# A two-layer hybrid block on one core: the first modulation in quarters and column groups, raw weights issued on ScalarE's queue, and a last tile whose second half comes in two parts

## The chip, the core and the metric

The kernel runs as one program on one core of a Trainium2 chip. Five engines work there from queues of their own, each in the order in which its instructions stand: TensorE (PE, with its weight loads as PEld), VectorE (DVE), ScalarE (ACT), GpSimd (POOL) and SyncE (SP). They wait for one another by semaphores. An instruction that waits holds everything behind it on its engine, and that goes for an instruction that issues a DMA too. The metric is the device time of one execution in microseconds (us). Before the change it is 3673.63 us, the median of three runs (3672.63 to 3673.88).

## The reference

Two layers (`DEPTH` 2) over 2048 latent and 256 context tokens of 1024 values each. Cut to what matters here:

```python
silu_c, silu_cc = jax.nn.silu(c), jax.nn.silu(c_ctx)
for l in range(DEPTH):
    mod_lat = silu_c @ w_ada[l] + b_ada[l]        # (1, 3*1024): shift, scale, gate
    mod_ctx = silu_cc @ w_ada[l] + b_ada[l]
    x, ctx = _layer(x, ctx, mod_lat, mod_ctx, ...)
return _rms_norm(x, g_final)

# _layer:
sh, sc, gt = jnp.split(mod_lat, 3, axis=-1)
xn = _rms_norm(x, g_norm) * (1 + sc[:, None]) + sh[:, None]
(au, av, az, bq, bk, bv, bz, cq, ck, cv, co, cz, cg) = _split_proj(xn @ w_in)
# gated MLP on (au, av, az), attention on (bq, bk, bv, bz), mLSTM on (cq, ck, cv, co, cz, cg)
x = x + gt[:, None] * (jnp.concatenate([y_a, y_b, y_c], axis=-1) @ w_out)
```

Nothing can be projected before the shift and the scale of layer 0 are known: they are two products of a vector of 1024 with 2048 columns of `w_ada[0]`, 8 MB in all.

## The kernel before, in words

The tokens are 18 tiles of 128 (2 of context, 16 latent). Per layer there are three phases: the projection (`proj_phase`, about 0 to 890 us and 1912 to 2680 us), the attention (`attn_phase`), and the output projection (`out_phase`, 1695 to 1912 us and from 3457 us). The instructions are written as Python generators; a scheduler that works with a timeline of its own then sets the order on each engine, so an edit moves instructions that it doesn't name.

**Projection.** Three macros of six tiles each; in each macro seven groups of columns of `w_in` (c1, c3, c2, a1, a2, b1, b2), 8 chunks of 128 rows per group (k = 0 to 7). A chunk is loaded as `raw` (three buffers, `wload`), and split into a rounded part and a rest (`split_w`, L197 to L204: CAST on ACT and subtraction on DVE, for a quarter of the chunks both on POOL) into one of 11 `w` buffers. A tile takes 24 matmuls of 512 columns per group (`gemm`, L209). Four of a group's eight `w` buffers come free halfway through the group's last tile. After its matmuls a tile is evacuated by ACT and DVE, and the results go to DRAM with `ld` on SP's queue; `put_blocks` writes a transposed block as four small DMAs (to `sct`, `sy`, `sk`, `sq`). Late in each projection phase the mLSTM (`ml_state`, `ml_out`) runs between the matmuls.

**All loads on one queue.** `ld` (L51 to L58) issues on SP: weights, tokens, `w_ada`, rope tables (`tab`), and nearly all stores.

**The first modulation.** `mod_load(0, h)` loads `w_ada[0]` in two halves h of 4 MB, eight DMAs of 512 KB each, into the later `xn` buffers. `mod_first(0, h)` multiplies: `silT` holds the two silu vectors, two columns per k. In half 0 the shift's columns are summed on DVE (`mod_sum`, L401 and L403) and the scale's on PE; in half 1 both are on PE (L384: 24 matmuls of 512 columns with a stationary operand of two columns, two profile records each). The rows are then copied, transposed back (L395) and finished by `mod_fin`. The first three tiles are normalised ahead (`make_xn`): per half, four transposes, then scale and shift of four blocks of 128 columns, CAST and subtraction.

**Other modulations.** `mod_job` sums `w_ada` of layer 1 and the gates on DVE, from 64 loads of 256 KB (`mst`, three buffers). These loads and the `tab` loads are written inside `tc.issue_after(lastw[0])`: they may not be put ahead of the last weight load that has been written, as far as both are on one engine.

**Output.** `out_phase` gives two matmul groups of 512 columns per tile; in the last layer then the gate, the residual, a Square with a sum, the inverse root on POOL (three instructions) and two multiplications on DVE, each followed by a store.

Of the kernel before, what the change touches and what calls it, by code (L numbers as in the profile page):

```python
# [12 lines left out]
ALU = mybir.AluOpType  # L13
# [22 lines left out]
def hybrid_kernel(ctx: ExitStack, tc: tile.TileContext, x, c, ctxt, c_ctx, w_ada, b_ada, g_norm, w_in, w_s, b_s,  # L36
# [135 lines left out]
    silT = const([P, KC, 2], "silT")  # L172
# [39 lines left out]
    def out_phase(l):  # L212
        last = l == DEPTH - 1

        with ExitStack() as st:
# [61 lines left out]
            for ti, i in enumerate(tiles):  # L277
# [7 lines left out]
                ss = pt([P, 2], "ss", 3) if last else None  # L285
                for g in range(2):
                    cs = slice(g * 512, (g + 1) * 512)
                    acc = pacc()
                    gemm(acc, xs, ws[g], 0, 512)
                    V.tensor_tensor(xnew[:, cs], acc, gt[s][:, cs], op=ALU.mult)  # L290
                    (V if last else G).tensor_tensor(xnew[:, cs], xnew[:, cs], xo[:, cs], op=ALU.add)
                    if last:
                        A.activation(xo[:, cs], xnew[:, cs], AF.Square, accum_out=ss[:, g:g + 1])
                if not last:
                    nc.gpsimd.dma_start(xres[i], xnew)
                else:
                    rs = pt([P, 1], "rs", 3)
                    G.tensor_tensor(rs, ss[:, 0:1], ss[:, 1:2], op=ALU.add)
                    rsqrt(rs, rs, 1.0 / D, EPS, 1)
                    for g in range(2):  # L300
                        cs = slice(g * 512, (g + 1) * 512)
                        V.scalar_tensor_tensor(xnew[:, cs], xnew[:, cs], rs, gfin[:, cs], op0=ALU.mult, op1=ALU.mult)
                        ld(out[0, (i - NCT) * P:(i - NCT + 1) * P, cs], xnew[:, cs])

    def proj_phase(l):
        with ExitStack() as st:
# [29 lines left out]
            def silu_prep():  # L336
# [9 lines left out]
                V.tensor_copy(silT, tr[:, 0:16].rearrange("p (s k) -> p k s", s=2))  # L346
# [19 lines left out]
            def mod_load(l, h):  # L366

                src = w_ada[l, :, 0:2 * D].rearrange("(k p) (g h c) -> k p g h c", p=P, g=2, h=2)
                for k in range(KC):
                    if k % 2 == 0:  # L370
                        t = xns[AHEAD + k // 2 % (half + 1 - AHEAD)]().bitcast(F32)
                        mraw.append(t.rearrange("p a k t -> p (a k t)").rearrange("p (q g c) -> p q g c", q=2, g=2))
                    raw = mraw[-1][:, k % 2]
                    gate[0] = ld(raw, src[k, :, :, h, :]).ins

            def mod_first(l, h, rT):

                tr = pm()
                accs = [pacc() for _ in range(1 + h)]
                vacc = [] if h else [pt([P, 520], "mkv", 3) for _ in range(2)]  # L380
                for k in range(KC):
                    raw = mraw[(h * KC + k) // 2][:, k % 2]
                    for j, acc in enumerate(accs):
                        T.matmul(acc[0:2], silT[:, k, :], raw[:, 1 - j], start=(k == 0), stop=(k == KC - 1))  # L384
# [905 lines left out]
```

## Time and profile before

| what | us |
|---|---|
| median of three runs | 3673.63 |
| the profiled execution | 3684.58 |
| its span, first to last instruction | 3682.9 |
| PE busy in the span | 3582.6 |
| DVE, ACT, POOL busy | 2556.9, 1942.0, 1892.3 |

The profiled execution is 10.95 us longer than the median of the runs, and 1.7 us of it lie outside the span. A line of the profile names the line of the code, the engine, the operation, and what it writes and reads (`out<-in`); an idle time is put down to what ended it. PE's busy time is modelled from the starts of pipelined matmuls, so that how far two matmuls start apart says more than how long one lasts. A matmul of full-precision operands (L384, L777, L830) leaves two records.

### The profile page before, as it was taken

How to read it: one execution, taken by the hardware profiler on the slowest of the kernel's cores; microseconds unless marked ns; L12 is line 12 of the kernel's file. 1: busy time of each engine (PE TensorE's matmuls, PEld its weight loads, DVE VectorE, ACT ScalarE, POOL GpSimd, SP SyncE). 2: the span in 40 equal slices, each digit the busy share in tenths (PEclk: the TensorE clock that was granted, in tenths of full speed). 3: DMA queues.
4: the chain of work that ended last, by engine and by line, in shares of the span. 5: the costliest groups of instructions: out<-in, count | busy, mean ns of one | idle time of the engine just before them, and what ended most of it. 6: DMA issues, size and time to landing. Idle time of an engine off the chain costs nothing.

```text
span 3682.9 us, 58371 instructions
## 1 busy us (share of the span) xinstructions
PE 3582.6 (97%) x19405; PEld 2937.3 (80%) x19405; DVE 2556.9 (69%) x6341; ACT 1942.0 (53%) x3409; POOL 1892.3 (51%) x2448
## 2 busy tenths in 40 slices
PE   8999999998999999999999999999999999999999
PEld 4877778776888888887788788877778888888787
DVE  4676664778888888887324636466888888888754
ACT  4223243334878788786114432432377877777621
POOL 2241342454777777776322524244557777777610
PEclk9999999999999999999999999999999999999999
DMA  7456455576001011002545553557720101100143
GB/s 216 137 138 175 138 129 136 159 194 156 25 28 37 17 35 43 24 12 95 175 121 151 132 148 83 141 145 180 174 57 18 31 27 35 35 24 10 58 148 113
DMA packets 531690, 359.21 MB, mean 98 GB/s; under 512 B 297274, under 2 KB 432178, under 8 KB 531388
## 3 DMA queue, kind: packets, MB, share of 16 engines
q1 hardware_dynamic: 518172, 336.05, 33.8%
q10 hardware_dynamic: 10368, 9.52, 0.8%
q0 software_dynamic: 2848, 9.91, 0.7%
q8 instruction: 154, 2.52, 0.3%
q14 instruction: 148, 1.21, 0.1%
HBM read 269.56 MB, written 85.76 MB: 96 GB/s over the span
## 4 chain that ended last, share of the span: by engine, by line
PE 69%; DMA 6%; DVE 4%; POOL 3%; issue 2%; SPq 2%; ACT 2%; DVEq 0%; POOLq 0%; ACTq 0%
PE acc L209 20%; PE m L1131 14%; PE acc L1096 14%; PE tr L1113 9%; PE x L209 6%; PE x L1113 4%; SPq L53 2%; DMA raw<-in_w_in_dram 1%; DMA xt<-snm 1%; DMA mkv<-sc 1%; DMA tab<-in_rope_dram 1%; DVE w L200 1%; DVE e L1098 1%; PE tr L476 0%; POOL pT L1120 0%
## 5 line engine op out<-in xcount | busy, mean ns | idle before, releaser
L209 PE MATMUL acc<-w,xn 128*128 128x512 f32 (+2 forms) x4728 | 1096.5, 385 | 5.3 <-POOL w L203 1.7
L209 PEld LDWEIGHTS acc<-w,xn 128*128 128x128 f32 x4728 | 844.2, 191 | 182.8 <-issue 5.4
L1098 DVE TENSOR_SCALAR_CACHE_REDUCE e<-acc,rqall 128x512 f32<-128x512 f32 (+1 forms) x1296 | 858.1, 690 | 144.4 <-PE acc L1096 76.6
L1131 PE MATMUL m<-pT,vst 128*128 128x512 f32 (+1 forms) x2336 | 775.3, 415 | 4.8 <-POOL pT L1120 4.0
L1096 PE MATMUL acc<-kst,qs 128*128 128x512 f32 (+1 forms) x2592 | 744.5, 385 | 11.6 <-DVE e L1098 10.0
L1120 POOL TENSOR_TENSOR pT<-pf,pT 128x512 fp32r<-128x512 f32 (+1 forms) x564 | 730.5, 1302 | 29.7
L1104 ACT ACTIVATE e<-e,nmx 128x2304 f32<-128x2304 f32 (+1 forms) x272 | 578.5, 2127 | 61.4 <-DVE nmx L1103 60.7
L1119 POOL TENSOR_SCALAR pT<-pf 128x512 fp32r<-128x512 f32 (+1 forms) x564 | 356.8, 636 | 338.5 <-ACT pf L1118 332.9
L1096 PEld LDWEIGHTS acc<-kst,qs 128*128 128x128 f32 x2592 | 447.4, 189 | 92.1 <-DVE e L1098 21.7
L1131 PEld LDWEIGHTS m<-pT,vst 128*128 128x128 f32 x2336 | 411.7, 189 | 65.6 <-POOL pT L1120 8.6
L1113 PE MATMUL tr<-ident,e 128*128 128x128 f32 x3084 | 456.9, 273 | 3.0 <-DVE pT L1123 2.1
L1113 PEld LDWEIGHTS tr<-ident,e 128*128 128x128 f32 x3084 | 375.1, 141 | 79.1 <-DVE pT L1123 4.0
L200 DVE TENSOR_TENSOR w<-raw,w 128x512 fp32r<-128x512 f32 (+1 forms) x276 | 205.5, 755 | 184.0 <-ACT w L199 182.3
L199 ACT CAST w<-raw 128x512 fp32r<-128x512 f32 (+1 forms) x276 | 161.6, 595 | 299.0 <-DMA raw<-in_w_in_dram 265.1
L1123 DVE TENSOR_TENSOR pT<-tr,pT 128x512 fp32r<-128x512 f32 x405 | 274.2, 683 | 59.5 <-ACT pT L1122 58.4
L209 PE MATMUL acc<-w,xs 128*128 128x512 f32 x1224 | 294.2, 398 | 1.7 <-DVE xs L249 1.3
L1122 ACT CAST pT<-tr 128x512 fp32r<-128x512 f32 x405 | 234.4, 587 | 95.2 <-PE tr L1113 79.8
L209 PEld LDWEIGHTS acc<-w,xs 128*128 128x128 f32 x1224 | 230.9, 189 | 58.3 <-DVE xs L249 1.7
L209 PE MATMUL x<-w,xn 128*128 128x512 f32 (+1 forms) x1128 | 263.3, 379 | 10.4 <-DVE w L200 6.0
L1118 ACT COPY pf<-tr 128x512 f32<-128x512 f32 (+1 forms) x372 | 214.5, 584 | 87.1 <-PE tr L1113 77.8
L202 POOL TENSOR_SCALAR w<-raw 128x512 fp32r<-128x512 f32 (+1 forms) x92 | 65.5, 712 | 361.7 <-PE acc L209 158.7
L209 PEld LDWEIGHTS x<-w,xn 128*128 128x128 f32 x1128 | 200.1, 190 | 54.8 <-DVE w L200 8.9
(282 smaller groups left out, 4402.9 us busy)
## 6 DMA issues: line engine op xcount, KB each, us to landing
raw<-in_w_in_dram SPq DMA_DIRECT2D x240, 256.0 KB, 3.1
raw<-in_w_in_dram SPq DMA_DIRECT2D x144, 128.0 KB, 2.4
mkv<-sc SPq DMA_DIRECT2D x68, 258.0 KB, 4.0
xt<-snm SPq DMA_DIRECT2D x68, 256.0 KB, 4.5
yr<-sy SPq DMA_DIRECT2D x34, 512.0 KB, 6.5
mst<-in_w_ada_dram SPq DMA_DIRECT2D x64, 256.0 KB, 3.7
qd<-sq SPq DMA_DIRECT2D x128, 128.0 KB, 2.8
xres<-xnew POOLq DMA_DIRECT2D x18, 512.0 KB, 5.2
```

The lines of the kernel that those rows point to most:

```text
L200: V.tensor_tensor(wt[:, 1, :n], raw[:, :n], wt[:, 0, :n].bitcast(F32), op=ALU.subtract)
L209: T.matmul(acc[:, :n], xs[:, a, k, :], ws[k][:, b, c0:c0 + n], start=(k == 0 and j == 0), stop=(k == KC - 1 and j == 2))
L1096: T.matmul(acc[:, 0:w], u['qs'][:, r, j * P:(j + 1) * P], kf[:, c0:c0 + w], start=(r == 0), stop=(r == 1))
L1098: V.tensor_scalar(e[:, c0:c0 + w], acc[:, 0:w], rqall[:, u['tiles'][j], u['h']:u['h'] + 1], None, op0=ALU.mult, op1=ALU.max, accum_out=mx[ ...
L1104: A.activation(e[:, 0:nk], e[:, 0:nk], AF.Exp, bias=nmx, scale=1.0, accum_out=u['den'][:, j:j + 1])
L1113: T.transpose(tr[:, j * P:(j + 1) * P], u['e'][j][:, s * P:(s + 1) * P], ident)
L1118: A.copy(pf[:, 0:w], tr[:, 0:w])
L1119: G.tensor_scalar(pt_[:, 0, 0:w], pf[:, 0:w], 1.0, 0.0, op0=ALU.mult, op1=ALU.add)
L1120: G.tensor_tensor(pt_[:, 1, 0:w], pf[:, 0:w], pt_[:, 0, 0:w].bitcast(F32), op=ALU.subtract)
L1122: A.copy(pt_[:, 0, 0:w], tr[:, 0:w])
L1123: V.tensor_tensor(pt_[:, 1, 0:w], tr[:, 0:w], pt_[:, 0, 0:w].bitcast(F32), op=ALU.subtract)
L1131: T.matmul(u['o'][:, 0:w], vst[u['g']][:, s, :], pt_[:, r, 0:w], start=(s == 0 and r == 0), stop=(s == u['nk'] - 1 and r == 1))
```

## The change

Three edits. (1) The first modulation comes in four quarters of 2 MB, each in eight DMAs of 256 KB; both the shift and the scale are on PE, with `silT` padded to 32 columns by zeros, so that four matmuls of 256 columns go to four groups of 32 columns of the array. A small matrix `sel`, built from the identity, adds the two groups that belong together while it transposes. The first three tiles are normalised by quarters too. (2) From the twelfth chunk of each layer on, the raw weights are issued on ACT's queue and no longer on SP's; with that, `issue_after(lastw[0])` names an instruction of another engine and no longer holds back the `mst` and `tab` loads on SP. (3) In the last tile of the last layer the second half of 512 columns comes as two parts of 256; the first half is multiplied by `g_final` on POOL ahead of time, and its last multiplication goes to ACT.

```diff
-    silT = const([P, KC, 2], "silT")
+    silT = const([P, KC, 32], "silT")
+    G.memset(silT, 0.0)
+    sel = const([P, 2, 2], "sel")
+    i4 = ident.rearrange("p (a b r) -> p a b r", a=2, b=2)
+    G.tensor_tensor(sel, i4[:, 0, :, 0:2], i4[:, 1, :, 0:2], op=ALU.add)
...
+                end = last and ti == len(tiles) - 1
+                parts = [(0, 512), (512, 256), (768, 256)] if end else [(0, 512), (512, 512)]
...
+                        if end and g == 0:
+                            G.tensor_tensor(xnew[:, cs], xnew[:, cs], gfin[:, cs], op=ALU.mult)
+                        if end and g == 1:
+                            G.tensor_tensor(ss[:, 0:1], ss[:, 0:1], ss[:, 1:2], op=ALU.add)
...
-                        V.scalar_tensor_tensor(xnew[:, cs], xnew[:, cs], rs, gfin[:, cs], op0=ALU.mult, op1=ALU.mult)
+                        if end and g == 0:
+                            A.mul(xnew[:, cs], xnew[:, cs], rs)
+                        else:
+                            V.scalar_tensor_tensor(xnew[:, cs], xnew[:, cs], rs, gfin[:, cs], op0=ALU.mult, op1=ALU.mult)
...
             def mod_load(l, h):
-                src = w_ada[l, :, 0:2 * D].rearrange("(k p) (g h c) -> k p g h c", p=P, g=2, h=2)
+                src = w_ada[l, :, 0:2 * D].rearrange("(k p) (g h c) -> p k g h c", p=P, g=2, h=4)
...
             def mod_first(l, h, rT):
+                acc = pm()
+                for k in range(KC):
+                    raw = mraw[(h * KC + k) // 4][:, k % 4]
+                    for j in range(2):
+                        o = (2 * k + j) % 4 * 32
+                        T.matmul(acc[o:o + 32, 0:256], silT[:, k, :], raw[:, j], start=(k < 2), stop=(k >= KC - 2))
+                rows = k1()
+                A.copy(rows, acc[:, 0:256])
                 tr = pm()
-                accs = [pacc() for _ in range(1 + h)]
-                vacc = [] if h else [pt([P, 520], "mkv", 3) for _ in range(2)]
...
-                        T.matmul(acc[0:2], silT[:, k, :], raw[:, 1 - j], start=(k == 0), stop=(k == KC - 1))
-                    mod_sum(vacc, raw[:, 0], k)
...
+                for q in range(2):
+                    T.matmul(tr[:, q * 4:q * 4 + 4], rows[:, q * P:(q + 1) * P], sel.rearrange("p j s -> p (j s)"),
+                             start=(q == 0), stop=(q == 1))
+                mod_fin(l, tr[:, 0:8].rearrange("p (k g s) -> p g s k", k=2, g=2), rT, h * 2, h * 2 + 2)
...
             def wload():
                 while len(wraw) < len(chunks) and len(wraw) < len(wt) + 3:
+                    q = ld if len(wraw) < 11 else nc.scalar.dma_start
                     raw = rawp.tile([P, 512], F32, tag="raw", name=nm("raw"))
                     for (a, o, w) in chunks[len(wraw)][0]:
-                        lastw[0] = ld(raw[:, o:o + w], a).ins
+                        lastw[0] = q(raw[:, o:o + w], a).ins
...
-                mod_first(0, 0, rT)
                 wload()
                 mod_load(0, 1)
+                mod_first(0, 0, rT)
                 for gen in xgens:
                     next(gen)
                     next(gen)
-                wtick(4)
-                mod_first(0, 1, rT)
-                for gen in xgens:
-                    run_all(gen)
+                for h in range(1, 4):
+                    wtick(2)
+                    if h < 3:
+                        mod_load(0, h + 1)
+                    mod_first(0, h, rT)
+                    for gen in xgens:
+                        next(gen, None)
                 wtick(12)
```

How the order moves, at three places. First SP's and ACT's queues where the second macro goes from group b1 to b2 (about 500 us in the trace of before). `sq` is b1's transposed store, in four pieces a tile, and the `raw` are the last chunks of b2. On SP, before:

```order
L53 DMA mkv_6018<-sc_123 128x516
L53 DMA sq_109<-k_756_4684 32x16x32 x2
L53 DMA dgt_0_218<-k_762_4727 1x512
L53 DMA sq_109<-k_763_4735 32x16x32 x4
L53 DMA sq_109<-k_767_4778 32x16x32 x4
L53 DMA raw_4859<-in_w_in_dram 128x512
L53 DMA raw_4864<-in_w_in_dram 128x512
```

On ACT, with the change, at the same place (L647 is the Square that evacuates a tile of b1, L205 the CAST of a chunk):

```order
L647 ACTIVATE k_764_4748<-acc_4717 128x512
L647 ACTIVATE k_771_4799<-acc_4761 128x512
L647 ACTIVATE k_775_4842<-x_4812 128x512
L647 ACTIVATE k_779_4885<-acc_4855 128x512
L205 CAST w_4920<-raw_4627 128x512
L205 CAST w_4925<-raw_4632 128x512
L961 DMA raw_4923<-in_w_in_dram 128x512
L961 DMA raw_4928<-in_w_in_dram 128x512
L205 CAST w_4935<-raw_4923 128x512
```

The two loads no longer stand behind the stores; they stand behind ACT's evacuations and the CASTs instead.

Second, DVE's queue with the change, from the third quarter's tiles on (`mkv<-mst` is a sum of `mod_job`, `mod<-m` the fourth quarter's `mod_fin`, `xn` the tiles' rest part):

```order
L500 TENSOR_TENSOR xn_334<-xt_331,xn_334 128x256
L496 TENSOR_SCALAR xt_340<-tr_545,mod_214 128x128
L500 TENSOR_TENSOR xn_343<-xt_340,xn_343 128x256
L412 TENSOR_SCALAR mkv_1039<-mst_1041,silT 128x512
L412 TENSOR_SCALAR mkv_1040<-mst_1041,silT 128x512
L414 SCALAR_TENSOR_TENSOR mkv_1039<-mst_1043,silT,mkv_1039 128x512
L414 SCALAR_TENSOR_TENSOR mkv_1040<-mst_1043,silT,mkv_1040 128x512
L414 SCALAR_TENSOR_TENSOR mkv_1039<-mst_1072,silT,mkv_1039 128x512
L414 SCALAR_TENSOR_TENSOR mkv_1040<-mst_1072,silT,mkv_1040 128x512
L206 TENSOR_TENSOR w_612<-raw_491,w_612 128x512
L378 TENSOR_TENSOR mod_214<-m_582,rT_310 128x2
```

Before, the first such sum stands on DVE behind the evacuations of group c3's first three tiles:

```order
L517 TENSOR_TENSOR gates<-acc_941,bgt 128x16
L517 TENSOR_TENSOR gates<-acc_981,bgt 128x16
L517 TENSOR_TENSOR gates<-x_1015,bgt 128x16
L401 TENSOR_SCALAR mkv_975<-mst_977,silT 128x512
L401 TENSOR_SCALAR mkv_976<-mst_977,silT 128x512
```

Six sums now stand ahead of the fourth quarter's `mod_fin`, 20 ahead of the fourth tile's `xn`, and 13 or 14 more ahead of the sixth tile's.

Third, PE's queue with the change, in the second quarter (`m_434` is its accumulator, L489 the tiles' transposes):

```order
L489 MATMUL tr_407<-ident,xt_340 128x128 x2
L400 MATMUL m_434<-xn_355,silT 32x256 x4
L489 MATMUL tr_462<-ident,xt_322 128x128 x2
L215 MATMUL acc_664<-w_414,xn_325 128x512 x2
L215 MATMUL acc_664<-w_419,xn_325 128x512 x3
L215 MATMUL acc_730<-w_414,xn_334 128x512
L400 MATMUL m_434<-xn_355,silT 32x256 x2
L215 MATMUL acc_730<-w_414,xn_334 128x512 x2
L215 MATMUL acc_730<-w_419,xn_334 128x512 x3
L400 MATMUL m_434<-xn_355,silT 32x256 x2
```

The modulation's matmuls come in runs of two to eight between full-width ones; before, L384 stood between them in the same way, in runs of two to eight.

## Rows read from the trace of the kernel before

**Rows 1.** The page, part 1: busy time, share of the span, instructions of each engine.
```profile
PE 3582.6 (97%) x19405; PEld 2937.3 (80%) x19405; DVE 2556.9 (69%) x6341; ACT 1942.0 (53%) x3409; POOL 1892.3 (51%) x2448
```
**Rows 2.** Busy us by stretch: PE, PEld, DVE, ACT, POOL, granted clock, DMA share, GB/s.
```profile
0.00:20.00 20.00, 12.43 (x20) 1.77 (x20) 11.39 (x24) 1.64 (x3) 6.26 (x21) 1.00 0.86 288
20.00:28.00 8.00, 4.58 (x32) 3.87 (x32) 5.11 (x13) 7.55 (x16) 5.73 (x8) 0.77 1.04 388
28.00:48.00 20.00, 20.00 (x54) 5.53 (x54) 6.84 (x12) 6.59 (x13) 4.43 (x6) 0.92 0.68 223
48.00:68.00 20.00, 17.77 (x86) 13.29 (x84) 8.34 (x23) 11.72 (x28) 2.42 (x6) 1.00 0.51 132
...
92.00:700.00 608.00, 584.76 (x2885) 478.32 (x2884) 378.49 (x831) 198.90 (x464) 213.04 (x294) 0.99 0.55 145
700.00:890.00 190.00, 174.81 (x1051) 138.48 (x1050) 146.94 (x395) 60.41 (x171) 94.33 (x133) 0.96 0.70 176
```
**Rows 3.** Timeline, 0 to 150 us: start, length, instruction; the first modulation.
```profile
14.75 4.06 DVE L403 SCALAR_TENSOR_TENSOR mkv<-xn,silT,mkv 128x512 f32<-128x512 f32 x6
...
36.19 7.03 PE L384 MATMUL acc<-xn,silT 128*2 128x512 f32 x16
```
**Rows 4.** Groups by form: count, busy us, mean ns of one, idle before.
```profile
L830 PE MATMUL tr<-msc,xt 128*128 128x65 f32 x352 | 49.3, 283 | 0.0
...
L384 PE MATMUL acc<-xn,silT 128*2 128x512 f32 x48 | 27.6, 724 | 2.4 <-DMA xn<-in_w_ada_dram 2.1 <-DVE silT L346 0.3
...
L777 PE MATMUL m<-m,mkv 128*64 128x65 f32 x544 | 29.6, 232 | 8.2 <-POOL k L600 2.9 <-DVE st L780 1.9 <-issue 1.8
```
**Rows 5.** Timeline of PE, 66 to 90 us: the sixth tile's c1, then c3.
```profile
82.76 7.43 PE L209 MATMUL acc<-w,xn 128*128 128x512 f32 x38
```
**Rows 6.** Waits of PE's weight loads, 60 to 700 us: total, times, longest.
```profile
PEld x L209 <- DVE w L200: 8.1, 6, 2.3
PEld x L209 <- ACT w L199: 5.5, 4, 2.4
...
PEld acc L209 <- POOL w L203: 2.1, 1, 2.1
```
**Rows 7.** Timeline of SP's DMA issues, 500 to 518 us.
```profile
502.13 9.67 SPq L53 DMA_DIRECT2D sq<-k  x10
511.90 5.30 SPq L53 DMA_DIRECT2D raw<-in_w_in_dram  x4
```
**Rows 8.** Timeline of ACT, 498 to 518 us.
```profile
514.99 0.62 ACT L199 CAST w<-raw 128x512 fp32r<-128x512 f32 x1 [8.56 <-DMA raw<-in_w_in_dram]
```
**Rows 9.** Timeline of PE, 505 to 518 us.
```profile
504.66 6.80 PE L209 MATMUL acc<-w,xn 128*128 128x512 f32 x29
...
515.87 1.66 PE L209 MATMUL acc<-w,xn 128*128 128x512 f32 x6 [1.69 <-POOL w L203]
```
**Rows 10.** Waits of ACT, 60 to 700 us: total, times, longest.
```profile
ACT k L526 <- DVE k L525: 65.0, 27, 9.1
...
ACT k L634 <- DMA sq<-k: 21.7, 3, 14.5
```
**Rows 11.** ACT's own DMA issues of one line: ns shortest, median, longest.
```profile
L495 ACTq DMA_DIRECT2D sc<-k x36: 326/326/353, 61.7 to 2378.4; - x36
```
**Rows 12.** The page, part 6: DMA issues, KB each, median us to landing.
```profile
raw<-in_w_in_dram SPq DMA_DIRECT2D x240, 256.0 KB, 3.1
```
**Rows 13.** DMA issues from 700 to 890 us.
```profile
raw<-in_w_in_dram SPq DMA_DIRECT2D x12, 256.0 KB, 6.3
```
**Rows 14.** Waits of PE's weight loads in layer 1, 1912 to 2450 us.
```profile
PEld x L209 <- ACT w L199: 1.1, 2, 0.7
```
**Rows 15.** Timeline, from 3660 us: the end of the last tile.
```profile
3675.10 0.69 DVE L290 TENSOR_TENSOR xnew<-acc,gt 128x512 f32<-128x512 f32 x1 [4.20 <-PE acc L209]
...
3676.55 0.63 ACT L293 ACTIVATE xo<-xnew 128x512 f32<-128x512 f32 x1 [4.76 <-DVE xnew L291]
...
3678.49 1.42 DVE L302 SCALAR_TENSOR_TENSOR xnew<-xnew,rs,gfin 128x512 f32<-128x512 f32 x2 [1.98 <-POOL rs L131]
```

More of the change, by code (lines that the diff above doesn't have):

```diff
@@ L366, in mod_load @@
             def mod_load(l, h):
-                src = w_ada[l, :, 0:2 * D].rearrange("(k p) (g h c) -> k p g h c", p=P, g=2, h=2)
+                src = w_ada[l, :, 0:2 * D].rearrange("(k p) (g h c) -> p k g h c", p=P, g=2, h=4)
                 for k in range(KC):
[L370 to L374, printed above, removed]
@@ L376, in mod_first @@
-            def mod_first(l, h, rT):
-                tr = pm()
-                accs = [pacc() for _ in range(1 + h)]
-                vacc = [] if h else [pt([P, 520], "mkv", 3) for _ in range(2)]
-                for k in range(KC):
-                    raw = mraw[(h * KC + k) // 2][:, k % 2]
-                    for j, acc in enumerate(accs):
-                        T.matmul(acc[0:2], silT[:, k, :], raw[:, 1 - j], start=(k == 0), stop=(k == KC - 1))
-                    mod_sum(vacc, raw[:, 0], k)
-                for s, acc in enumerate(vacc):
-                    for q in range(4):
-                        T.matmul(tr[:, q * 2 + s:q * 2 + s + 1], acc[:, q * P:(q + 1) * P], ones[:, 0:1],
-                                 start=True, stop=True)
-                for j, acc in enumerate(accs):
-                    row = k2()
-                    A.copy(row[0:2], acc[0:2])
-                    for q in range(4):
-                        c0 = (1 - j) * 8 + q * 2
-                        T.transpose(tr[:, c0:c0 + 2], row[0:2, q * P:(q + 1) * P], ident[0:2, 0:2])
-                mod_fin(l, tr[:, 0:16].rearrange("p (g k s) -> p g s k", g=2, s=2), rT, h * 4, h * 4 + 4)
+                    if k % 4 == 0:
+                        n = h * 2 + k // 4
+                        t = xns[AHEAD + n % (half + 1 - AHEAD)]().bitcast(F32)
+                        mraw.append(t.rearrange("p a k t -> p (a k t)").rearrange("p (q g c) -> p q g c", q=4, g=2))
@@ L451, in proj_phase, with make_xn @@
             xs = {}
-            def make_xn(i, slack=True, halves=False):
+            def make_xn(i, slack=True, quarters=False):
                 s = 1 if i < NCT else 0
@@ L472, in make_xn @@
                 xf = xt.rearrange("p (k t) -> p k t", k=KC)
-                for b in range(2):
+                nb = 4 if quarters else 2
+                w = KC // nb
+                for b in range(nb):
                     tr = ptr()
-                    for k in range(4):
-                        T.transpose(tr[:, k * P:(k + 1) * P], xf[:, b * 4 + k, :], ident)
-                    for k in range(4):
-                        kk = b * 4 + k
-                        if k < 3:
+                    for k in range(w):
+                        T.transpose(tr[:, k * P:(k + 1) * P], xf[:, b * w + k, :], ident)
+                    for k in range(w):
+                        kk = b * w + k
+                        if k < w - 1:
                             A.activation(xf[:, kk, :], tr[:, k * P:(k + 1) * P], AF.Identity,
@@ L955, in wtick @@
                     wload()
-            xgens = [make_xn(i, halves=first) for i in macros[0][:AHEAD]]
+            xgens = [make_xn(i, quarters=first) for i in macros[0][:AHEAD]]
             if first:
```

20 lines of the change are left out of this document (11 added, 9 removed).

## The prediction

> **What bounds the kernel now.** The first view is the page's busy times: PE works 97% of the span, no other engine over 69% [rows 1]. So an edit counts only where PE stands still, runs at the low clock, or does work that falls away. The second view, the busy time by stretch, says where that is [rows 2]: from 0 to about 48 us PE's work before the projection is the first modulation, at a granted clock of 0.77 and 0.92 of full speed in two stretches; in 92 to 700 us PE is busy 584.76 of 608, and the other 23.2 us are waits; in 700 to 890 us 15.2 us are idle. The third view, the waits of PE's weight loads, names part of these 23.2: weights whose split is late on DVE, ACT and POOL, 8.1 + 5.5 + 2.1 = 15.7 us in 60 to 700 us [rows 6]. One such wait can be followed through three timelines: SP issues ten pieces of `sq` in 9.67 us and only then, at 511.90, the next raw weights [rows 7]; ACT has waited 8.56 us for them when it casts at 514.99 [rows 8]; PE waits 1.69 us for a weight at 515.87 [rows 9]. Last, the tail: after the last matmul the chain is serial over DVE, ACT, POOL and DVE [rows 15].
>
> **Edit 1, the prologue.** Removed are the 16 first sums on DVE, 4.06 / 6 = 0.68 us each [rows 3], and the 48 full-width modulation records on PE (24 matmuls of two records). A run of them takes 7.03 / 16 = 0.44 us a record [rows 3], so the second half, 32 records, takes 14.1 us. Added are 128 records of 256 columns, 96 of them in the last three quarters; a half-width record is estimated at half, 0.22. If the column groups run one after the other, the 96 take 21 us, 7 more than the 32 before; if two run at once, 10.5; if four do, 5.3. Nothing in the trace shows four. It shows two: L777, 64 columns wide, has 544 records in 29.6 us, 54 ns each, where L830, as short, has 352 in 49.3, 140 ns each [rows 4]. I take two at once for the sum; PE then saves some 4 us here, but it isn't PE that ends the prologue, as follows.
>
> The Trainium skill speaks against this edit: the page "TensorEngine Tiling (Array Packing)", section Key Properties, says that changing the tiling mode drains TensorE, while tiles of one mode work independently. The order shows runs of two to eight group matmuls between full-width ones, so the mode would change again and again; no row here prices one. By the independence rule alone the 96 records would take 5.3 us, by the drain rule more than that, by an amount that the page doesn't give.
>
> What decides is when the loads are in and what DVE has to do then. All 8 MB must come in before as after; but the third quarter's end decides now about less remaining work. Up to the third quarter's last DMA the new order issues 32 raw-size DMAs of 0.262 MB, 3 of 0.524 and 6 of 0.262, in all 11.5 MB. At 288 GB/s to 20 us (5.76 MB), 388 GB/s to 28 us (3.10 MB) [rows 2], the remaining 2.7 MB come in by about 34.9 us, and the first `mst` loads behind them by 36.9. From there DVE has a chain. Since `issue_after` no longer holds the `mst` loads, 20 sums of `mod_job` stand ahead of the fourth tile's `xn`, 20 x 0.68 = 13.6 us; the other DVE work there I take as the 8.3 us that DVE does in 48 to 68 us [rows 2], with three weight subtractions (about 0.69 each, as any 128x512 pass [rows 15]) and the fourth tile's own pieces, 2 us each: 12.7 us. That is 36.9 + 26.3 = 63. Then 13 sums more, 8.8 us, and 6 us of other work (8.34 / 20 of the time [rows 2]) bring the sixth tile's `xn` to 78 us. Before, its c1 began at 82.76 [rows 5], so PE arrives 4.8 us earlier at the point from which it runs without gaps. With the clock's part (0.08 of 20 us at 28 to 48 us [rows 2], 1.6 us, of which I take 1.2 back) this edit gives **-6.0**. The ends: if the sums do not stand in the way (DVE then has 22 us less ahead of it), PE itself becomes the limit and the term is about -14 (the whole run of 14.1 us); if each of some ten `mst` loads makes DVE wait 1 us beyond that, +5.
>
> **Edit 2, raws on ACT's queue.** 404 of the 464 raw loads leave SP; the last stores no longer stand ahead of them. Each costs ACT 0.326 us of issue [rows 11], 132 us in all, on an engine busy 53% [rows 1]; that lies beside PE, as far as no chain through ACT is late. Of the 15.7 us of weight waits in layer 0, those whose raw stood behind stores go, and the others (a split late because DVE or ACT was busy) stay. The timelines show the first kind for the one that I followed; I take half: **-8.0**. The ends: all 15.7, and 0. In layer 1 there is little to win, the largest group of weight waits is 1.1 us [rows 14]: 0. In the mLSTM stretch 12 raw issues leave SP in 700 to 890 us [rows 13]; at about 0.4 us each that frees 5 us of SP's time of 190, and of 15.2 us idle on PE I take a tenth in each layer: **-3.0** for both, ends 0 and -15.
>
> New are the waits on ACT: a raw now stands behind ACT's waits. The tightest place is the boundary of a group. Eight of 11 `w` buffers are in use and three are made ahead; halfway through the last tile four come free, and the chunk with k = 6 needs the raw buffer of k = 3. After halfway: CAST 0.62 [rows 8], subtraction 0.69 [rows 15], issue 0.33 [rows 11], landing 3.1 [rows 12], CAST and subtraction again, 6.05 us in all. PE needs that weight after 12 matmuls of the tile and 18 of the next group, 30 x 6.80 / 29 [rows 9] = 7.0 us. So there is 1.0 us of slack for the wait that stands ahead of the raw on ACT. Those waits are 65.0 / 27 = 2.4 us in the mean, the longest of one line 14.5 [rows 10]; but few of them fall on a raw at a boundary. I charge **+2.0** (at 1.4 us beyond the slack, one or two boundaries of 42, three macros by seven groups by two layers); the ends are 0 and the slower rival below.
>
> A page bears on this: "Trainium Kernel Development and Optimization", section Key Constraints, says that DMAs issued from several engines run on the same 16 DMA engines, and that this saves only issue time. The DMA share of 0.55 in 92 to 700 us [rows 2] leaves room, and what the raw waited for [rows 7] was issue time, so by row and rule the gain of this edit is what was lost to issuing and no more.
>
> **Edit 3, the tail.** The gate and residual of the last part are on 256 columns: 0.69 each [rows 15] become about half, -0.65. The Square, 0.63, loses about 0.2 (part of it is fixed). The two last multiplications, 1.42 together on DVE [rows 15], go to ACT and DVE side by side, about -0.5. Against that stands a second matmul group's start. **-1.3**, between 0 and -2.
>
> **Sum.** -6.0 - 8.0 - 3.0 + 2.0 - 1.3 = -16.3 us, against the profiled execution of 3684.58, that is 3668.3. The median of the runs is 10.95 us below that execution, so 3657 for it.
>
> **Rivals.** (a) *Bigger gain:* the issues on SP are what holds the mLSTM stretch. For it: 15.2 us of idle PE there [rows 2], and a landing of 6.3 us against 3.1 elsewhere [rows 12, 13]. Against: only 12 of the many issues there move. If half the idle goes in both layers, 15 instead of 3: 3645.
> (b) *No change:* the sums of `mod_job`, released early, hold the sixth tile back by what the quarters win, and the weight waits return from three raw buffers rather than from the queue. For it: 33 sums ahead of that tile; DVE, not a raw, ends most of the weight waits [rows 6]. Against: those DVE waits follow late raws where I traced one. Left are the tail and some of the stretch at 700 us: about 3670.
> (c) *Slower:* the raws are held on ACT. An evacuation that waits for DVE keeps the issue of a raw back at each boundary by 2.4 us against a slack of 1.0, so 1.4 us a boundary. At half of the 42 boundaries +29; prologue and tail keep -7.3: 3695. It decides from six boundaries on. For it: 27 such waits in 640 us [rows 10], and the order, in which four evacuations stand directly ahead of two CASTs and the raws. Against: before, the CAST that releases the buffer stood behind the same evacuations, and the raw behind the CAST; that wait isn't new, only that SP's store queue is no longer in series with it.
>
> **How the numbers follow.** The forecast has 0.50, (a) 0.16, (b) 0.21, (c) 0.13. A difference of 0.2%, 7.3 us, is about what a measurement can tell from no change. The forecast and (a) are faster, with a fifth of (b) at its better end: 0.70. The rest of (b) is the same: 0.17. Slower is (c): 0.13. The range goes from 3638 (beyond (a), with a prologue near its better end) to 3683 (a light case of (c)); it leaves out most of (c) and a little of (a).
>
> **What would show it.** In the new profile: SP issues no raw after the first ones, and weight waits in 60 to 700 us fall from 15.7 to about 8; no CAST waits for a raw for 8 us behind stores. The sixth tile's c1 begins near 78 us; DVE in 37 to 63 us does sums of `mod_job`. Matmuls of the modulation start in overlapping pairs, 0.11 us apart on average; fours would start 0.06 apart, serial ones 0.22. From the last matmul to the end it is 1.3 us shorter. Wrong it would be if PE's weight waits stay or grow with ACT named as the releaser and a raw's issue behind an evacuation, or if the sixth tile starts after 82 us, with DVE in sums or waiting for `mst`.

## The result, and the profile after

The changed kernel takes 3644.07 us (median of 6 runs, 3638.64 to 3652.2) against 3673.76 for the kernel before: the ratio is 0.9908, with an interval of 0.9897 to 0.9919. That is some 30 us less by the medians, 34 by the ratio and 30 to 38 by its interval, where 16.3 were forecast. A second comparison gave 0.9911 (0.9897 to 0.9926), with 3641.52 us. The direction was right, the time lies inside the stated range, but the size is off by a factor of about two, and the working was wrong in its two largest terms. One execution of a kernel below is left out: of six with the order edge away for `mst` alone, one took 8984.5 us.

Busy time by stretch of the changed kernel, columns as in [rows 2]:

```profile
20.00:28.00 8.00, 6.93 (x25) 3.51 (x25) 5.56 (x10) 2.90 (x7) 2.90 (x4) 0.50 1.09 349
28.00:48.00 20.00, 20.00 (x135) 11.63 (x135) 9.02 (x31) 6.49 (x16) 3.77 (x6) 0.99 0.87 277
48.00:68.00 20.00, 15.53 (x76) 10.71 (x75) 16.88 (x40) 8.20 (x20) 3.67 (x6) 0.86 0.75 225
68.00:92.00 24.00, 20.31 (x99) 17.31 (x100) 19.69 (x36) 14.36 (x34) 2.44 (x4) 0.83 0.87 219
92.00:700.00 608.00, 607.14 (x3035) 492.96 (x3033) 376.97 (x866) 208.35 (x482) 226.93 (x322) 1.00 0.56 146
700.00:890.00 190.00, 177.22 (x990) 137.63 (x989) 150.22 (x415) 72.34 (x186) 88.75 (x124) 0.91 0.69 174
```

Two rows carry the story. From 92 to 700 us PE is busy 607.14 of 608 us instead of 584.76 [rows 2]: nearly all of its idle time is gone there, and the granted clock is 1.00. From 48 to 68 us it is the other way round: PE loses 4.5 us, where it lost 2.2, DVE is busy 16.88 us instead of 8.34, and the granted clock is 0.86 instead of 1.00.

The waits of PE's weight loads, 60 to 700 us (total, times, longest). In the kernel before, two rows belong beside the three of [rows 6]:

```profile
PEld acc L209 <- DVE w L200: 1.7, 2, 1.1
...
PEld acc L209 <- ACT w L199: 1.5, 1, 1.5
```

In the changed kernel:

```profile
PEld tr L489 <- DVE xt L496: 4.5, 1, 4.5
...
PEld acc L215 <- ACT w L205: 1.8, 3, 0.9
...
PEld acc L215 <- DVE w L206: 0.4, 1, 0.4
```

Of 18.9 us of waits for weights (15.7 and these two rows) 2.2 are left. The longest wait is now for the fourth tile's scaling (L496), which stands on DVE behind four sums, two normalisations and a wait of 0.72 us for POOL. In the timeline of PE the modulation's matmuls in column groups, and the sixth tile's c1 followed by c3, against [rows 3, 5]:

```profile
34.21 1.93 PE L400 MATMUL m<-xn,silT 128*32 128x256 f32 x32
...
43.95 0.62 PE L400 MATMUL m<-xn,silT 128*32 128x256 f32 x4
44.50 0.44 PE L489 MATMUL tr<-ident,xt 128*128 128x128 f32 x2
...
71.69 1.97 PE L489 MATMUL tr<-ident,xt 128*128 128x128 f32 x8 [4.13 <-DVE xt L496]
...
90.05 7.38 PE L215 MATMUL acc<-w,xn 128*128 128x512 f32 x37
```

32 records in 1.93 us are 60 ns each; in the run without column groups (below) single ones of the same width take 0.22 us. So four groups do run at once. But only these 32 come in one long run. A burst of four between full-width matmuls takes 0.55 us to the next start (43.95 to 44.50), 0.31 more than 4 x 60 ns, and the 96 records of the last three quarters take 10.5 us together. And c1 of the sixth tile begins at 90.05 us, not at 82.76 and not at the forecast 78; a start after 82 us was one of the prediction's signs of being wrong.

What the prediction hadn't read is a view of the kernel before: what DVE waited for, 100 to 600 us (of the same columns):

```profile
DVE mkv L403 <- DMA mst<-in_w_ada_dram: 30.4, 22, 3.6
...
DVE mkv L401 <- DMA mst<-in_w_ada_dram: 9.7, 4, 4.3
```

And in the changed kernel:

```profile
DVE mkv L414 <- DMA mst<-in_w_ada_dram: 7.4, 10, 2.2
```

DVE stood 40.1 us before sums of `mod_job` whose load was late, and everything behind them on DVE, the weights' subtractions among it, stood too. One place of it, on DVE in the kernel before:

```profile
103.43 0.88 DVE L401 TENSOR_SCALAR mkv<-mst,silT 128x512 f32<-128x512 f32 x2 [4.30 <-DMA mst<-in_w_ada_dram]
104.23 4.15 DVE L403 SCALAR_TENSOR_TENSOR mkv<-mst,silT,mkv 128x512 f32<-128x512 f32 x4
108.30 0.16 DVE L517 TENSOR_TENSOR gates<-acc,bgt 128x16 f32<-128x16 f32 x1
108.38 2.73 DVE L403 SCALAR_TENSOR_TENSOR mkv<-mst,silT,mkv 128x512 f32<-128x512 f32 x4
...
111.34 0.75 DVE L403 SCALAR_TENSOR_TENSOR mkv<-mst,silT,mkv 128x512 f32<-128x512 f32 x1 [0.15 <-DMA mst<-in_w_ada_dram]
112.01 0.69 DVE L200 TENSOR_TENSOR w<-raw,w 128x512 fp32r<-128x512 f32 x1
```

and on PE:

```profile
112.75 0.97 PE L209 MATMUL x<-w,xn 128*128 128x512 f32 x3 [1.75 <-DVE w L200]
```

The first sum waits 4.30 us for its load, eleven sums go through nearly without a break, and only then comes the subtraction that PE waits 1.75 us for. No raw load is late here: ACT's CASTs of these chunks began at 104.14 and 105.21. The next raw is late because of it: SP issues it at 112.73, when the subtraction has left the raw buffer, and ACT waits 8.46 us for it.

### The profile page after: what moved, and what is told of

Same layout as the page of the kernel before. It is cut to its first block, busy times and chain, and to the rows that moved or that the text cites. A ratio compares the mean times of both kernels' runs of the same rounds, so it can differ in the third digit from the quotient of the medians.

```text
span 3643.3 us, 58460 instructions
## 1 busy us (share of the span) xinstructions
PE 3569.5 (98%) x19497; PEld 2933.0 (81%) x19497; DVE 2552.6 (70%) x6350; ACT 1943.8 (53%) x3413; POOL 1894.5 (52%) x2452
## 4 chain that ended last, share of the span: by engine, by line
PE 82%; DMA 5%; DVE 5%; POOL 2%; issue 2%; ACT 2%; SPq 2%; ACTq 0%; POOLq 0%; DVEq 0%
PE acc L215 30%; PE m L1149 14%; PE acc L1114 14%; PE tr L1131 9%; PE x L215 8%; PE x L1131 4%; SPq L53 2%; DMA xt<-snm 1%; DMA raw<-in_w_in_dram 1%; DMA xt<-in_x_dram 1%; DVE w L206 1%; DMA mkv<-sc 1%; PE tr L489 1%; DVE e L1116 1%; DMA vr<-sv 0%
## 5 line engine op out<-in xcount | busy, mean ns | idle before, releaser
L215 PE MATMUL acc<-w,xn 128*128 128x512 f32 (+2 forms) x4728 | 1110.2, 387 | 6.3 <-DVE k L611 2.8
L1122 ACT ACTIVATE e<-e,nmx 128x2304 f32<-128x2304 f32 (+1 forms) x272 | 578.2, 2126 | 59.3 <-DVE nmx L1121 58.3
L206 DVE TENSOR_TENSOR w<-raw,w 128x512 fp32r<-128x512 f32 (+1 forms) x276 | 213.0, 781 | 155.4 <-ACT w L205 147.7
L215 PE MATMUL acc<-w,xs 128*128 128x512 f32 (+1 forms) x1248 | 300.6, 395 | 1.8 <-ACT xs L254 1.1
L205 ACT CAST w<-raw 128x512 fp32r<-128x512 f32 (+1 forms) x276 | 161.2, 594 | 255.2 <-DMA raw<-in_w_in_dram 170.8
L215 PE MATMUL x<-w,xn 128*128 128x512 f32 (+2 forms) x1128 | 254.7, 373 | 0.0
L1131 PE MATMUL x<-ident,e 128*128 128x128 f32 x1556 | 235.9, 273 | 1.8 <-DVE pT L1141 1.6
```

Source lines behind the costliest of these rows:

```text
L206: V.tensor_tensor(wt[:, 1, :n], raw[:, :n], wt[:, 0, :n].bitcast(F32), op=ALU.subtract)
L215: T.matmul(acc[:, :n], xs[:, a, k, :], ws[k][:, b, c0:c0 + n], start=(k == 0 and j == 0), stop=(k == KC - 1 and j == 2))
L1122: A.activation(e[:, 0:nk], e[:, 0:nk], AF.Exp, bias=nmx, scale=1.0, accum_out=u['den'][:, j:j + 1])
L1131: T.transpose(tr[:, j * P:(j + 1) * P], u['e'][j][:, s * P:(s + 1) * P], ident)
```

## The experiments

Since executions of one kernel differ by some 10 us from run to run, the places are compared in profiles, by the start of the n-th record of a projection matmul (L209 before), counted from 0. "Before" is here a second profile of it (span 3678.6; the first had 100.4, 159.8 and 545.1). The last column is the ratio to the kernel before with its interval, which is safer than a difference of two medians, since each group of runs has a kernel before of its own (3671.91 to 3677.35 us).

| kernel | 240th | 500th | 2000th | 500th to 2000th | ratio |
|---|---|---|---|---|---|
| before, again | 99.7 | 158.6 | 542.2 | 383.6 | |
| edit 3 alone | 99.0 | 157.8 | 540.8 | 383.0 | 0.9996 (0.9987 to 1.0006) |
| edit 1 alone | 99.2 | 159.6 | 538.6 | 379.0 | 0.9963 (0.9950 to 0.9977) |
| edit 1 without column groups | 107.0 | 165.5 | 540.8 | 375.3 | 0.9956 (0.9941 to 0.9970) |
| edit 2 alone | 109.0 | 163.6 | 526.6 | 363.0 | 0.9922 (0.9909 to 0.9935) |
| edit 2, layer 0 only | 108.9 | 163.5 | 527.8 | 364.3 | 0.9929 (0.9915 to 0.9944) |
| order edge away, raws on SP | 108.6 | 163.2 | 528.4 | 365.2 | 0.9953 (0.9940 to 0.9967) |
| edge away for `mst` only | 107.7 | 162.3 | 524.8 | 362.5 | 0.9947 (0.9931 to 0.9963) |
| edge away for `tab` only | 99.8 | 158.1 | 533.0 | 374.9 | 0.9971 (0.9957 to 0.9985) |
| stores on ACT | 100.3 | 157.0 | 545.3 | 388.3 | 0.9974 (0.9960 to 0.9988) |
| before, thin sums | 100.7 | 157.9 | 529.0 | 371.1 | 0.9967 (0.9955 to 0.9979) |
| changed | 106.6 | 162.2 | 522.0 | 359.8 | 0.9908 (0.9897 to 0.9919) |
| changed, again | 106.0 | 161.6 | 522.7 | 361.1 | 0.9911 (0.9897 to 0.9926) |
| changed, raws on SP, no edge | 107.4 | 162.9 | 523.5 | 360.6 | 0.9924 (0.9909 to 0.9940) |
| changed, `mst` held | 99.1 | 163.5 | 528.4 | 364.9 | 0.9917 (0.9904 to 0.9930) |
| changed, thin sums | 104.0 | 159.5 | 519.3 | 359.8 | 0.9898 (0.9882 to 0.9914) |

Where the projection is the same, the times from the 500th to the 2000th agree to some 2 us: 383.0 to 385.3 in three profiles (before twice, edit 3 alone), 359.8 and 361.1 for the changed kernel. But every other edit lets the scheduler order the rest anew. Edit 1 alone, with and without column groups, is 4.6 and 8.3 us shorter there, although it touches neither the edge nor a queue; a difference of that size is not yet a cause.

**The kernel before, again.** 

> The kernel before, unchanged, for a second profile of it. The first profiled execution took 3684.58 us, 10.9 us over the median of the runs. If that excess lies in the waits for weights (a matter of how the stores and raw loads happen to meet on SP's queue), this profile shows fewer than 36.9 us of PE's lost time in 100 to 600 us and some 3674 us in all; if it is spread over the whole span, the lost time there is the same and the difference lies in the attention.

 It took 3680.3 us; PE's lost time in 100 to 600 us (the time by which matmuls start later than the median distance of like ones: idle and slow clock) was 34.3 us, in the first profile 36.8. So the waits are no accident of one execution, and the second profile is the better one to compare with.

**Each edit alone.** The diffs are those of the three edits.

> Edit 2 alone: raw loads from the twelfth chunk on ScalarE's queue, with the mst and tab loads no longer held back. Theory A (nearly all of the gain is the weights, which now never come late): 25 to 30 us faster, about 3646, waits of PE's weight loads on w under 3 us in 60 to 700 us. Rival B (the edits share the gain as forecast, and the profile of before overstates the waits): 9 to 15 us faster, about 3661. Rival C (the issue order of the sums costs as much as the weights win in the first 140 us): 15 to 20 us faster, with the sixth tile's c1 later than 82.76 us.

 3647.60 us against 3676.62: theory A in size, with rival C's late prologue in it as well; the waits for weights in 60 to 700 us are 8.5 us, not under 3 as A had it. The 240th matmul is 9.3 us later than before, and the 2000th 15.6 us earlier.

> Edit 1 alone: quarters and column groups, raw loads and mst as before. Theory A (the prologue lost in the changed kernel only because the sums of mod_job stand in DVE's way; here they are held): 5 to 9 us faster, about 3667, the sixth tile's c1 near 74 to 78 us. Rival B (the quarters themselves win nothing: PE's full-width matmuls wait for the same last bytes): within 3 us of before.

 3664.72 us: the 240th matmul is only 0.5 us earlier, so the prologue itself wins nothing that shows (B), although the whole kernel is about 12 us faster (14 by the ratio). The gain is made later: 3.6 us are there by the 2000th matmul, and the rest comes behind it. No edit stands there; but the scheduler sets the order of the rest anew, and what in it makes the gain stays open.

> Edit 3 alone: the last tile's second half in two parts. Forecast -1.3 us, bounds 0 and -2; with the noise of the median, 3671 to 3674. A rival: the part of 256 columns costs PE more than it saves the tail, 0 to +1 us.

 3674.78 us: not to be told from no change, as the interval (-4.8 to +2.2 us) holds the forecast.

**Which part of edit 2.** The edge is the `issue_after` of the `mst` and `tab` loads.

```diff
-                    with tc.issue_after(lastw[0]):
+                    if True:
                         ld(raw[:, 0:512], w_ada[l, k * P:(k + 1) * P, grp * 512:(grp + 1) * 512])
...
-                with tc.issue_after(lastw[0]):
+                if True:
                     ld(tab, rope[:, i - NCT])
```

> Before, with only the order edge of the mst and tab loads taken away; the raw loads stay on SP. Theory A (the weight waits come from raws that stand behind stores on SP, and the freed sums only cost): the sixth tile's first matmuls 7 to 9 us later as with edit 2 alone, PE's lost time in 100 to 600 us still over 28 us, total the same to +8 us, 3674 to 3684. Rival B (DVE, relieved later because the sums are done early, ends the waits): lost time in 100 to 600 us under 15 us, and 12 to 20 us faster.

 3662.69 us: rival B. Raws still stand behind the same stores on SP, and yet 18.4 of the 383.6 us between the 500th and the 2000th matmul are gone, nearly as many as with edit 2 (20.6). The explanation of the prediction, raws stuck behind stores, is refuted as the main cause of what is won there. Of the whole gain of edit 2 alone this is about half (14.7 of 29.0 us by the medians); of the 14.7 us by which the two profiles differ, 12.9 come behind the 2000th matmul.

```diff
-                    q = ld if len(wraw) < 11 else nc.scalar.dma_start
+                    q = ld if len(wraw) < (11 if l else 32) else nc.scalar.dma_start
```

> The changed kernel, with the raw loads of layer 0 on SP up to the 32nd chunk instead of the 11th, which holds the mst loads back as before; later raws on ScalarE's queue. Theory A (the freed sums cost the prologue 6 to 8 us, and the later gain does not need them): 5 to 9 us faster than the changed kernel, about 3637, at 100 us PE no later than in the kernel with edit 1 alone. Rival B (the sums have to be done some time and cost PE the same later): within 3 us of the changed kernel, 3641 to 3647.

 3646.70 us: rival B. The prologue is 7.5 us earlier than in the changed kernel at the 240th matmul and has given it back by the 500th (163.5): 35 sums stand between the two, where DVE works 28.1 us on them and waits 16.4 for their loads.

```diff
-            ld(rows.rearrange("(b r) t -> r b t", r=32)[:, :, o], t[o].rearrange("r (b c) -> r b c", c=32))
+            nc.scalar.dma_start(rows.rearrange("(b r) t -> r b t", r=32)[:, :, o], t[o].rearrange("r (b c) -> r b c", c=32))
```

> Before, with the four-piece stores of put_blocks on ScalarE's queue; raw loads and the order edge as before. Theory A (what matters is that no raw stands behind these stores): lost time in 100 to 600 us falls from 34 to under 15 us, 10 to 20 us faster, unless the stores, which wait for DVE, hold ScalarE's casts. Rival B (it is SP's whole issue load, not these stores): under 6 us faster.

 3667.13 us, about 10 us faster, but not by theory A: the lost time in 100 to 600 us was 37.8 us, no less than before. 16.0 of them were lost at 200 to 250 us alone, where ACT (L526) waits 11.5 us for stores of `sk`, as it never does there in the kernel before. What is left, 21.8 us, is less than before: the run doesn't decide on the stores.

```diff
-                    q = ld if len(wraw) < 11 else nc.scalar.dma_start
+                    q = ld if l or len(wraw) < 11 else nc.scalar.dma_start
```

> Edit 2 in layer 0 alone; in layer 1 the raws stay on SP. Theory A (layer 1 had no weight waits to lose, so that the gain is in layer 0 but for the mLSTM stretch): 20 to 24 us faster than before, 4 to 7 us of edit 2's gain missing. Rival B (all of the gain is in layer 0): the same as edit 2 alone, 28 us.

 3650.40 us, 3 us over edit 2 alone, within the uncertainty of both. Nearly all of the gain comes with the raws of layer 0; but the profiles show in its place a part of what theory A had missing, the mLSTM stretch of layer 1, which takes 269.8 us here and 264.2 with edit 2 in both layers.

**Which of the two loads, and what is left for the queue.** The edge of one load taken away, as above; then the changed kernel with all raws on SP.

> Before, with the order edge taken from the mst loads alone. Theory A (late mst loads held DVE, and the weights' subtractions behind the sums): most of the 14.7 us that the whole edge gave, 10 to 15 us faster; DVE's waits for mst in 100 to 600 us fall from 40 to some 12 us, lost time there from 34 to under 20 us. Rival B (the tab loads do it): within 4 us of before, since the sums cost the prologue 9 us and win little later.

 3651.73 us (median of five) against 3671.91: theory A, with somewhat more than its 10 to 15 us. DVE's waits for `mst` fall to 10.8 us:

```profile
DVE mkv L403 <- DMA mst<-in_w_ada_dram: 10.8, 13, 3.0
```

At the place shown above the sums have long been done, and DVE waits for ACT alone:

```profile
111.37 0.17 DVE L517 TENSOR_TENSOR gates<-acc,bgt 128x16 f32<-128x16 f32 x1 [2.86 <-ACT k L516]
112.00 1.71 DVE L200 TENSOR_TENSOR w<-raw,w 128x512 fp32r<-128x512 f32 x2 [0.45 <-ACT w L199]
```

and PE runs on:

```profile
104.69 9.28 PE L209 MATMUL acc<-w,xn 128*128 128x272 f32 x72
113.81 2.45 PE L209 MATMUL x<-w,xn 128*128 128x512 f32 x10
```

> Before, with the order edge taken from the tab loads alone. Theory A (it is the mst loads): within 4 us of before. Rival B (the tab loads, bunched behind raws, delayed the rope multiplications and so the burst of sq stores ahead of the raws at 500 us): 8 to 15 us faster, the sums still held, the prologue as before (within 1 us at 100 us), no weight wait near 510 us.

 3661.68 us: rival B holds too: the sums are still held, the 240th matmul is where it was, and from 490 to 530 us PE waits for no weight. Freeing the `tab` loads by themselves goes with 8.7 us between the 500th and the 2000th matmul, no more than the new order gave in edit 1 without column groups. The two loads don't add up: 21.1 and 8.7 us alone, 18.4 together.

> The changed kernel with all raw loads on SP's queue again, but without the order edge. Theory A (the queue itself matters still for the mLSTM stretches, out_phase and layer 1, as between the two runs of edit 2 and of the edge alone): 8 to 15 us slower than the changed kernel, 3652 to 3659. Rival B (the edge is all): within 4 us of it, 3640 to 3648.

 3646.39 us, against 3644.07 and 3641.52 for the changed kernel: rival B. In the full kernel the queue of the raws is worth 2 to 5 us by the medians and 5 to 6 by the ratios once the edge is gone, and the intervals overlap. Without edits 1 and 3 the same step gives 11 us by the ratios (0.9953 to 0.9922). So the edits don't add up: one by one their ratios make 44 us, together 34.

```diff
-                        o = (2 * k + j) % 4 * 32
-                        T.matmul(acc[o:o + 32, 0:256], silT[:, k, :], raw[:, j], start=(k < 2), stop=(k >= KC - 2))
+                        T.matmul(acc[0:2, j * 256:j * 256 + 256], silT[:, k, :], raw[:, j],
+                                 start=(k == 0 and j == 0), stop=(k == KC - 1 and j == 1))
```

> Edit 1 alone, in quarters but without column groups: a stationary operand of two columns, matmuls of 256 columns one after the other into two halves of one accumulator, transposed with the identity. Theory A (PE is not what ends the prologue, but the loads and then DVE and ACT): within 4 us of edit 1 alone, 3661 to 3669. Rival B (four at once matter): 128 records at 0.2 us instead of 0.06, of which the 96 of the later quarters cost 10 to 14 us, 3675 to 3679.

 3655.64 us: theory A for the time, as no loss shows. But rival B is right on the place: the 240th matmul is 7.8 us later than with column groups, as the single records are longer:

```profile
36.71 6.21 PE L388 MATMUL m<-xn,silT 128*2 128x256 f32 x28
```

The kernel wins that back later, for reasons the runs don't show. So a late prologue need not make the whole later.

**Waits or work.** The sums keep their place and their waits, but all except the first of each group are 16 columns wide, so that the modulation of layer 1 and the gates are not computed in full.

```diff
-                        V.scalar_tensor_tensor(acc[:, 0:512], raw, silT[:, k, s:s + 1], acc[:, 0:512],
+                        V.scalar_tensor_tensor(acc[:, 0:w], raw[:, 0:w], silT[:, k, s:s + 1], acc[:, 0:w],
...
-                    mod_sum(accs, raw[:, 0:512], k)
+                    mod_sum(accs, raw[:, 0:512], k, 16)
```

> Before, with the sums of mod_job (all but the first of each group) over 16 columns instead of 512: the modulation of layer 1 and the gates are not computed in full, and every load, wait and instruction stays. Theory A (DVE waits for late mst loads, and what is queued behind it is late): the waits stay, 4 to 8 us faster at most, lost time in 100 to 600 us over 25 us. Rival B (the duration of the sums fills DVE in 100 to 500 us): lost time there under 12 us, 14 to 20 us faster, as with the mst loads freed.

 3664.49 us: between the two. DVE waits even longer for `mst`,

```profile
DVE mkv L403 <- DMA mst<-in_w_ada_dram: 52.4, 41, 3.6
DVE mkv L401 <- DMA mst<-in_w_ada_dram: 10.3, 7, 3.6
```

and still 12.5 us go between the 500th and the 2000th matmul. Counted in that stretch alone: the sums on DVE, its time on them and its waits for their loads:

| kernel | sums | busy us | waits for `mst` us | 500th to 2000th |
|---|---|---|---|---|
| before, again | 85 | 64.3 | 23.5 | 383.6 |
| edge away for `tab` only | 85 | 65.2 | 25.3 | 374.9 |
| before, thin sums | 82 | 24.8 | 41.9 | 371.1 |
| edge away for `mst` only | 77 | 59.3 | 10.8 | 362.5 |
| changed | 77 | 60.9 | 7.4 | 359.8 |

So freeing the `mst` loads doesn't take the sums out of the projection: 77 of 85 are still there. Ahead of the 240th matmul there are now 35, where there were none; in between there are none, where there were 28. What falls in the stretch is mainly the waiting. With the `mst` loads freed DVE spends 17.7 us less on sums and their waits, and PE gains 21.1; with thin sums 21.1 us less, and PE gains 12.5. So sums that hold DVE do cost PE time, but that isn't all: what the loads' new places on SP and the new order add, these runs don't part.

> The changed kernel with the same 16-column sums (modulation of layer 1 and gates not in full). Theory A (the early sums hold the sixth tile back, by DVE time): the 240th projection matmul 7 to 10 us earlier than in the changed kernel, that is at or before the time of the kernel before, and 4 to 8 us faster in all. Rival B (the waits for mst or the loads set it): the 240th matmul within 3 us of the changed kernel, total the same.

 3637.42 us. The 240th matmul is 2.6 us earlier than in the changed kernel, 4.3 later than before: B at that place. The duration of the sums explains under half of what the prologue lost (2.6 of 6.9 us). In this run PE waits there for a token tile, whose load stands among the early `mst` loads:

```profile
67.31 1.97 PE L489 MATMUL tr<-ident,xt 128*128 128x128 f32 x8 [4.91 <-DVE xt L479]
```

> The changed kernel once more, beside the two with thin sums: a ratio of 0.991 to the kernel before, 3642 to 3648.

 0.9911, 3641.52 us: as before.

No version that computes the whole result beats the changed kernel by more than the uncertainty; by the run with thin sums, their duration still costs it about 4 us.

## Why the prediction was wrong, point by point

**Edit 2's weight waits, -8.0, is the step that failed most.** "Those whose raw stood behind stores go, [...] I take half" was a cause read from one place (511 us) and taken for all. It didn't even belong to the largest row: what PE waited for there was a chunk of POOL's (515.87 [rows 9]), the only wait in the row of 2.1 us, and of the 8.1 us behind DVE none was followed. Rival (b)'s "those DVE waits follow late raws where I traced one" fits only the next wait in that place, 0.68 us at 518.20. Between the 500th and the 2000th matmul the changed kernel is 23.8 us faster than before. Without any raw leaving SP 18.4 us of that appear, with the `mst` loads freed alone 21.1. What the prediction had listed only as a cost, the freed `mst` loads, was the main gain: before, DVE waited 40.1 us for them in 100 to 600 us, and the weights' subtractions behind the sums waited too. Rival (b) read DVE rightly as the releaser of the largest row in [rows 6], but who held DVE wasn't asked; its own waits would have said it. The term was also bounded too low: the 15.7 are most of the waits for weights and nothing else, and with the other waits and the slow clock behind them PE lost 34.3 us in 100 to 600 us, of which 6.0 are left.

**Edit 1's prologue, -6.0, had the wrong sign in the changed kernel.** At the 240th matmul that is 6.9 us late, and edit 1 alone 0.5 early. The sums ahead of the fourth and the sixth tile were counted (36.9 to 63 to 78 us), and the chain's length was about right, but it starts later. The prediction let it begin with the loads at 36.9 us; on DVE the first sum stands behind the third quarter's tiles:

```profile
45.43 0.43 DVE L500 TENSOR_TENSOR xn<-xt,xn 128x256 fp32r<-128x256 f32 x1 [0.47 <-ACT xn L499]
45.77 0.88 DVE L412 TENSOR_SCALAR mkv<-mst,silT 128x512 f32<-128x512 f32 x2
```

So it begins 8.9 us late, and the fourth tile's `xn` (L500) comes at 72.32 us, 9.3 later than the forecast 63, though DVE takes 26.6 us for this part of the chain, as forecast (26.3). The end at +5, "if each of some ten `mst` loads makes DVE wait", was nearer in size, but not by its reason: from 28 to 92 us DVE waits 2.6 us for `mst`. (The 12.7 us of other DVE work in that chain add up to 12.4.) Of the late start 3.3 us are won back by the 500th matmul, as these sums need not be done later. On PE the 96 records take 10.5 us, what the prediction put down for two groups at once, though long runs show four: the bursts between full-width matmuls make the difference. The 32 records of the second half took 15.5 us before, so PE saves 5.0 us, where some 4 were taken; without column groups the 96 take 23.2. On the Trainium skill's two rules ("TensorEngine Tiling (Array Packing)", Key Properties): that tiles work independently agrees with the 60 ns; with a drain at each change of mode the 0.31 us that a burst of four takes beyond 4 x 60 ns would agree, but no run here parts a drain from the last matmul's own time. In the whole time edit 1 alone gives about 14 us, of which the prologue shows nothing.

**The mLSTM stretches, -3.0, were undersized.** From the first matmul of the mLSTM to the first of the attention it took 279.0 us before (second profile), 272.9 after; in layer 1 266.8 and 263.2: 9.7 us in both. The reason given, issues that leave SP, holds in layer 1 alone. In layer 0 the stretch takes 271 to 276 us in fourteen of the seventeen profiles, raws on SP or not (272.6 in the changed kernel with raws on SP); the other three have the projection of before (278 to 279). In layer 1 it takes 259 to 264 us in the six profiles of kernels that take raws or stores off SP there, and 265 to 272 in the other eleven. Behind the projection another 5.0 us go between the attention of layer 0 and the mLSTM of layer 1, which no term had; their cause stays open.

**The new waits on ACT, +2.0,** didn't show: PE waits 2.2 us for weights in all, and the slower rival (c), at 1.4 us a boundary, didn't occur.

**The tail, -1.3.** The last two multiplications stand side by side as forecast, against [rows 15]:

```profile
3636.25 0.42 DVE L299 TENSOR_TENSOR xnew<-acc,gt 128x256 f32<-128x256 f32 x1 [1.73 <-PE acc L215]
...
3638.96 0.72 ACT L316 ACTIVATE xnew<-xnew,rs 128x512 f32<-128x512 f32 x1 [1.28 <-POOL rs L131]
3638.96 0.75 DVE L318 SCALAR_TENSOR_TENSOR xnew<-xnew,rs,gfin 128x512 f32<-128x512 f32 x1 [1.83 <-POOL rs L131]
```

From the start of the last gate multiplication to the start of the last two it is 2.71 us (3638.96 - 3636.25) where it was 3.39 (3678.49 - 3675.10), and the last stage is 0.75 instead of 1.42 long: 1.35 us up to there. To the end of the span only 0.70 are left (7.08 us from that gate multiplication, where it was 7.78). Before, SP issued the first half's store at 3679.27, beside the second multiplication; now both stores come at the end, from 3639.71 on, a step that the term didn't have. The whole times can't resolve it.

**The rivals.** (a) gave 3645, close to what came, but that is luck: its stretch has a third of the gain at most, and only its layer 1 goes with the issues on SP. (b) was right that the freed sums hold the prologue, and wrong that nothing else would come of them.

Against the second profile (3678.6 to 3643.3, 35.3 us) the account is: up to the 500th matmul +3.6, from there to the 2000th -23.8, to the end of layer 0's projection -5.4, attention +1.5, to the mLSTM of layer 1 -5.0, its mLSTM stretch -3.6, the rest -2.6.

## What to carry to other kernels

When an engine in order is named as the one that makes another wait, read that engine's own waits and queue before explaining it. An edit that moves a load to another queue can lift an ordering rule that was written for the old one; price what this frees by the waits that it ends, not only by the work that comes earlier. A cause read from one wait is a sample of one: count how many of the waits in the row have it.

## What had not been expected of the hardware

Issuing 404 loads of 256 KB or less from ACT's queue instead of SP's is worth only 2 to 6 us in the full kernel (11 us by the ratios without edits 1 and 3), although SP waited 82.6 us in 100 to 600 us before for the split of an earlier chunk, as these rows of SP's waits before show (total, times, longest):

```profile
SPq L53 <- DVE w L200: 59.6, 34, 19.7
SPq L53 <- POOL w L203: 23.0, 15, 2.8
```

Matmuls in four groups of 32 columns start 60 ns apart in a run of 32, where single ones of the same width start 0.22 us apart; in bursts of four between full-width matmuls they take 0.14 us each.
